# A two-layer encoder kernel: layer 1's side work spread differently over engines, queues and buffers

## The chip, the cores and the metric

The kernel runs on one core of a Trainium2 chip. The metric is the device time of one execution in microseconds (us); lower is better. Engines are named as in the profile: PE is TensorE's matmuls, PEld its weight loads, DVE is VectorE, ACT ScalarE, POOL GpSimd, and SP is SyncE, which here only issues DMAs; a "q" behind a name (SPq, ACTq) is the engine's own queue of such issues.

## The reference

The program is a trunk of two layers on x of shape 1 x 2048 x 1024. Layer 0 mixes two attentions (dilated and differential); the change does not touch it. Layer 1 is, cut to what matters:

```python
h = rms_norm(x, norm_g) * (1 + scale) + shift
q, k, v, g = split(h @ w_in, [1024, 1280, 1536])       # w_in: 1024 x 2560
y = banded_attention(q, k, v)                          # 16 heads, 4 key heads, |i-j| <= 128, sink logit, ALiBi
x = x + gate * ((y * silu(g)) @ w_out)
out = rms_norm(x, final_g)
```

Everything is float32. Each product of two float32 operands is made of three matmuls in a reduced format: an operand is split into a high part and a low part (the rest), and high x high, high x low and low x high are summed.

## The kernel before, in words

**Stages of layer 1.** The 2048 tokens are four blocks (b = 0 to 3) of 512, or 16 tiles (t) of 128. For a block, `layer1_norm` loads x, normalises it, `layer1_h` transposes it in eight chunks of 128 features (k = 0 to 7; L1083) and `modulate` (L267) makes the high and low halves of h: ACT evicts the transposed chunk from PSUM with scale and shift (hr, L271), POOL writes the high part (L272), DVE the low part (L273). `layer1_qkv` (L1096) then projects in 11 pieces: two of k, one of v, eight of q; `layer1_gate` (L1109) has eight pieces of the gate. `proj_pieces` (L331) is a Python generator that gives control back after every step; for a k, q or gate piece a step is one chunk k, that is the three matmuls of `three` (L292) over 512 columns.

**Weights.** Each piece loads its 128 columns of w_in (`wr`, two buffers), ACT writes the high part (L342) and DVE, or POOL for odd pieces, the low part (L343). The v piece has 256 columns in two halves, both with the low part on POOL (L352). One piece is prepared ahead.

**Sinks.** A finished k or q piece goes through `split` (ACT high, DVE low) into tiles of the tag `ev` (four buffers) and is stored to HBM by two DMAs on SP (L397); v through L434 to L436, also into `ev`; the gate through a tanh on ACT and a DVE multiply, stored to `G1[b]` (L426).

**Attention** is done by tile t: `load_attend` brings K, V and Q back from HBM on SP (L1145 to L1159). A tile has four groups of four heads: scores (L603, L604), row maximum on DVE (L1184) and its product with the slope (nm, L1188), exp on ACT (L1191); then, one group later, transposes (L1199), the split of the transposed weights into hC and lC (for the middle key tile on POOL, L1206 and L1207, else ACT and DVE) and the products with V (L1219). At a tile's end y is scaled: a row of factors goes through HBM (L1249, L1252), POOL multiplies all of y in one instruction (L1254), and SP stores it to `yC[t]` (L1255).

**Order on TensorE.** Within this stage TensorE's order is written out by hand (`tc.manual_schedule`); the other engines' orders come from the framework's planner, which works from the order of the program and a simulated time. Each third of a head group is followed by some steps of a generator `filling`, at a rate that spreads n steps over the tiles (`parts_of`, L1326). While tiles of block b are attended, the filling is the gate of block b, then h and qkv of block b+1. `next_block` (L1310) orders the latter:

```python
next(norm)
for _ in norm:
    yield
    next(qkv)
    yield
```

so each transposed chunk is followed by the first qkv piece's matmuls on it. For block 3 the filling is its gate, then the gate of block 0, whose h is reloaded from HBM (16 loads, L1115); 76 steps of these 128 are spread over the attention, the rest comes behind it. PSUM has two buffers for transposes and projections together (`psj`, tag `mm`). h tiles have 20 buffers of the tag `hk`, where a block needs 16.

**Output.** `layer1_out` (L1057) goes through t = 0 to 15: y and G1 are loaded (L1004, L1006), multiplied on POOL (L1007), split, and multiplied with w_out, whose high and low halves stay in SBUF. w_out is loaded in 256 KB pieces (`load_wout`, L972): two chunks during the last attention tile, the other six (`wor1b`, `wor1c`) when the first output tile asks for them, on SP. The first two tiles take their terms in three parts, for the weights come in that order. Then the residual, the last norm and the store.

Of the kernel before, what the change touches and what calls it, by code (L numbers as in the profile page):

```python
# [21 lines left out]
P = 128  # L22
# [12 lines left out]
def f32(ap):  # L35
    return ap.bitcast(F32)
# [45 lines left out]
def tile_encoder(ctx: ExitStack, tc: tile.TileContext, x, c, ada_w, ada_b, norm_g, ab_w_in, ab_w_out,  # L82
# [248 lines left out]
    def proj_pieces(pool, ps, w, h, b, pieces, name, ahead=0):  # L331
# [4 lines left out]
        def weights(n):  # L336
            c0, sink_T, _ = pieces[n]
            if sink_T is not None:
                wr = pool.tile([P, KC, P], F32, name=f"wr_{name}_{b}_{n}", tag="wraw", bufs=2)
                nc.sync.dma_start(wr, w[:, c0:c0 + P].rearrange("(k p) f -> p k f", p=P))  # L340
                wt = pool.tile([P, 2, KC, P], FR, name=f"wt_{name}_{b}_{n}", tag="wt", bufs=2)
                nc.scalar.activation(wt[:, 0], wr, AF.Copy)  # L342
                (nc.gpsimd if n % 2 else nc.vector).tensor_tensor(wt[:, 1], wr, f32(wt[:, 0]), op=OP.subtract)  # L343
                return wt
            hi = pool.tile([P, KC, CH], FR, name=f"wh_{name}_{b}_{n}", tag="wt", bufs=2)
            lo = pool.tile([P, KC, CH], FR, name=f"wl_{name}_{b}_{n}", tag="wt", bufs=2)
            for i in range(2):
# [4 lines left out]
                nc.gpsimd.tensor_tensor(lo[:, ks], wr, f32(hi[:, ks]), op=OP.subtract)  # L352
# [40 lines left out]
    def sink_heads(pool, dst, scale, name, classes=None):  # L393
# [663 lines left out]
    def layer1_out(pool, ps, w, parts):  # L1057
        fg = row_bcast(pool, final_g.rearrange("(a d) -> a d", a=1), "fg")

        def finish(t, xt):  # L1060
# [6 lines left out]
                 by_k(lambda t: G1[t // 4][:, t % 4 * P:(t % 4 + 1) * P]), x1d, finish)  # L1067
# [15 lines left out]
    def layer1_h(pool, ps, b, xs, h, keep):  # L1083

        for k in range(KC):
            for part in h:
                part.append(pool.tile([P, 512], FR, name=f"h1T{b}_{len(part)}_{part is h[1]}", tag="hk", bufs=20))
# [8 lines left out]
    def layer1_qkv(pool, ps, h, b, qs):  # L1096
# [7 lines left out]
        pieces = [(D + f * P, sink_heads(pool, k_rows(f), 1.0, f"kc{f}"), None) for f in range(2)]  # L1104
        pieces.append((D + CH, None, sink_v(pool, lambda t: vC[b][t % 4 * P:(t % 4 + 1) * P], 64, "vc")))
        pieces += [(f * P, sink_heads(pool, q_rows(f), qs[:, f:f + 1], f"qc{f}"), None) for f in range(8)]
        return proj_pieces(pool, ps, c_w_in, h, b, pieces, "l1", 1)

    def layer1_gate(pool, ps, h, b):  # L1109
        if h is None:  # L1110
            h = [[pool.tile([P, 512], FR, name=f"h1G{b}_{i}_{k}", tag="hk", bufs=20) for k in range(KC)]
                 for i in range(2)]
            for k in range(KC):
                for i in range(2):
                    nc.sync.dma_start(f32(h[i][k]), hD1[i, :, k])  # L1115
# [47 lines left out]
    def attend(pool, ps, t, V, consts, loaded):  # L1163
# [73 lines left out]
        def end():  # L1237
# [16 lines left out]
            nc.gpsimd.tensor_tensor(y, y, F, op=OP.mult)  # L1254
            nc.sync.dma_start(yC[t], y)  # L1255
# [15 lines left out]
    with sbuf("pO") as pool_:  # L1271
# [8 lines left out]
        with sbuf("pO2") as pool2, psum("psO") as ps_:  # L1280
# [4 lines left out]
            pj = Bufs(right.enter_context(sbuf("pJ", side="right")), ev=4, wraw=2)  # L1285
# [14 lines left out]
    with sbuf("pC") as pool, psum("psC") as ps_:  # L1300
# [3 lines left out]
        with tc.manual_schedule(engines={nc.tensor.engine}):  # L1304
# [5 lines left out]
            def next_block(b):  # L1310

                h, xs = [[], []], layer1_norm(pj, b)
                norm, qkv = layer1_h(pj, psj, b, xs, h, False), layer1_qkv(pj, psj, h, b, qs)

                def go():
                    next(norm)
                    for _ in norm:
# [24 lines left out]
            for b in range(TB):  # L1342
                ts = range(max(4 * b - 1, 0), 4 * b + 3 if b < TB - 1 else NT)
                fills, n = [], 0
                if 0 < b < TB - 1:
                    fills, n = [layer1_gate(pj, psj, h1, b)], 64
                if b + 1 < TB:
                    h2, go = next_block(b + 1)
                    fills.append(go)
                    n += 8 + 96  # L1350
# [3 lines left out]
                filling, at = chain(*fills), [0, 0]  # L1354
# [23 lines left out]
    with sbuf("pZ") as pool, psum("psZ") as ps_:  # L1378
# [36 lines left out]
```

## Time and profile before

| | us |
|---|---|
| median of three runs | 3093.2 |
| lowest and highest run | 3083.75, 3102.27 |
| the profiled execution's own time | 3081.09 |
| its span, first to last instruction | 3079.2 |
| busy in the span: PE, DVE, ACT, POOL | 2789.2, 1947.1, 1495.6, 1141.1 |
| mean granted TensorE clock, of full speed | 0.964 |

The profile is of one execution; its rows give times from the start of the span. "busy" is the time in which an engine worked on an instruction. A matmul counts as busy also when the clock is halved, so a stretch loses time in two ways: PE idle, and PE busy at a granted clock under 1.00 (full speed is 2.4 GHz, the other level 1.2 GHz).

### The profile page before, as it was taken

What the parts mean: (1) busy time and instruction counts of PE and PEld (TensorE: products, weight loads), DVE (VectorE), ACT (ScalarE), POOL (GpSimd) and SP (SyncE); (2) the same over time, 40 slices, a digit from 0 to 9 for tenths busy, and PEclk for the clock granted to TensorE, in tenths of its full rate; (3) what the DMA queues carried; (4) which work ended last, traced back from release to release, by engine and by line L of the source; (5) the groups of instructions that cost most, each with busy time, mean ns of one, the idle gap of its engine ahead of it and who ended that gap; (6) DMA issues with size and microseconds to landing.
All of it is one profiled execution on the core that took longest, in us unless ns stands there. A gap on an engine that the chain in (4) does not pass through costs nothing. (4 is left out here: it accounts for less than half of the span.)

```text
span 3079.2 us, 43802 instructions
## 1 busy us (share of the span) xinstructions
PE 2789.2 (91%) x15056; PEld 2349.6 (76%) x15056; DVE 1947.1 (63%) x4248; ACT 1495.6 (49%) x2841; POOL 1141.1 (37%) x755
## 2 busy tenths in 40 slices
PE   6999799999999998899898888998898998988898
PEld 6788788888888887677776666786786886876686
DVE  7425276777776688755556766534685674777476
ACT  5311255556555556455556762222565664666221
POOL 3200175654746544222424332322333333344221
PEclk9999999999999999999999898999999998999899
DMA  6687743654645550398777888787677675875554
GB/s 262 235 284 237 204 135 103 195 168 134 168 141 175 132 183 21 100 266 227 208 215 196 202 240 244 248 279 179 175 191 179 184 181 145 201 169 162 176 192 161
DMA packets 545624, 577.00 MB, mean 187 GB/s; under 512 B 31521, under 2 KB 420858, under 8 KB 539258
## 3 DMA queue, kind: packets, MB, share of 16 engines
q1 hardware_dynamic: 533562, 557.43, 63.2%
q10 hardware_dynamic: 11840, 16.78, 1.6%
q8 instruction: 119, 1.95, 0.3%
q14 instruction: 103, 0.84, 0.1%
HBM read 405.98 MB, written 168.08 MB: 186 GB/s over the span
## 5 line engine op out<-in xcount | busy, mean ns | idle before, releaser
L654 ACT ACTIVATE s<-s,nm 128x2048 f32<-128x2048 f32 x128 | 256.7, 2006 | 141.4 <-DVE nm L653 141.3
L660 POOL TENSOR_SCALAR s<-s,rr 128x1536 f32<-128x1536 f32 x64 | 122.4, 1913 | 342.8 <-DVE rr L658 237.3
L603 PE MATMUL pq<-kB,q 128*128 128x512 f32 x512 | 217.0, 424 | 31.4 <-DVE mx L648 17.9
L675 ACT ACTIVATE th<-pt 128x512 fp32r<-128x512 f32 x256 | 146.9, 594 | 176.6 <-PE pt L671 137.4
L663 POOL TENSOR_TENSOR s<-s,s 128x1536 f32<-128x1536 f32 x64 | 230.2, 3596 | 4.9
L1184 DVE CUSTOM_DVE_ANT_0 sC<-pqC,tabC,isl 128x384 f32<-128x384 f32 (+1 forms) x256 | 148.9, 596 | 112.9 <-PE pqC L604 111.6
L604 PE MATMUL pq<-kB,q 128*128 128x512 f32 x512 | 206.1, 402 | 0.0
L676 DVE TENSOR_TENSOR tl<-pt,th 128x512 fp32r<-128x512 f32 x256 | 170.4, 683 | 53.2 <-ACT th L675 53.0
L648 DVE CUSTOM_DVE_ANT_0 s<-pq,ndist 128x1024 f32<-128x1024 f32 x128 | 156.0, 1219 | 75.5 <-PE pq L604 53.9
L1191 ACT ACTIVATE sC<-sC,nmC 128x384 f32<-128x384 f32 (+1 forms) x256 | 152.2, 596 | 90.7 <-DVE nmC L1188 90.2
L648 DVE CUSTOM_DVE_ANT_0 s<-pq,ndist,mx 128x1024 f32<-128x1024 f32 x128 | 163.5, 1277 | 28.0 <-PE pq L604 25.3
L297 PE MATMUL py<-tl,vB 128*128 128x256 f32 x512 | 151.8, 297 | 14.4 <-DVE tl L676 13.8
L671 PE MATMUL pt<-ident,s 128*128 128x128 f32 x1024 | 152.4, 276 | 2.7 <-DVE s L661 2.3
L294 PE MATMUL py<-th,vB 128*128 128x256 f32 x512 | 149.8, 292 | 2.1 <-ACT th L675 2.0
L343 POOL TENSOR_TENSOR wt_g<-wr_g,wt_g 128x1024 fp32r<-128x1024 f32 x32 | 77.4, 2418 | 199.0 <-ACT wt_g L342 194.4
L294 PE MATMUL pp_l<-h1T_False,wt_l 128*128 128x512 f32 x320 | 135.2, 423 | 17.2 <-POOL h1T_False L272 13.1
L603 PEld LDWEIGHTS pq<-kB,q 128*128 128x128 f32 x512 | 98.7, 193 | 63.7 <-DVE mx L648 28.8
L298 PE MATMUL py<-th,vB 128*128 128x256 f32 x512 | 146.2, 285 | 0.0
L1007 POOL TENSOR_TENSOR yr<-yr,gr 128x512 f32<-128x512 f32 (+1 forms) x46 | 61.3, 1335 | 206.1 <-issue 49.3
L1199 PE MATMUL ptC<-ident,sC 128*128 128x128 f32 x736 | 115.4, 277 | 19.5 <-ACT sC L1191 19.1
L298 PE MATMUL pp_l<-h1T_False,wt_l 128*128 128x512 f32 x320 | 127.6, 399 | 5.1 <-POOL wt_l L343 5.1
L297 PE MATMUL pp_l<-h1T_True,wt_l 128*128 128x512 f32 x320 | 128.3, 401 | 4.2 <-DVE h1T_True L273 4.1
(417 smaller groups left out, 9128.6 us busy)
## 6 DMA issues: line engine op xcount, KB each, us to landing
wr_a<-in_ab_w_in_dram SPq DMA_DIRECT2D x48, 512.0 KB
wr_l<-in_c_w_in_dram SPq DMA_DIRECT2D x48, 512.0 KB
hD<-h0T SPq DMA_DIRECT2D x8, 2048.0 KB
aw_ss<-in_ada_w_dram SPq DMA_DIRECT2D x32, 512.0 KB
hs_a<-hD SPq DMA_DIRECT2D x16, 1024.0 KB
q<-qB SPq DMA_DIRECT2D x128, 128.0 KB
wr_g<-in_ab_w_in_dram SPq DMA_DIRECT2D x32, 512.0 KB
hs_g<-hD SPq DMA_DIRECT2D x16, 1024.0 KB
```

Source lines behind the costliest of these rows:

```text
L294: first = nc.tensor.matmul(pt, l[0], r[0], start=(k == 0), stop=False)
L297: nc.tensor.matmul(pt, l[0], r[1], start=False, stop=False)
L298: nc.tensor.matmul(pt, l[1], r[0], start=False, stop=(k == nk - 1))
L603: first = nc.tensor.matmul(ps_, q0, k0, start=True, stop=False)
L604: nc.tensor.matmul(ps_, q1, k1, start=False, stop=True)
L648: nc.vector.tensor_tensor_reduce(out=s_[:, half * 1024:(half + 1) * 1024], in0=pq, in1=ndist[:, o:o + 1024], scale=1.0, scalar=LOW if half ...
L654: nc.scalar.activation(s_, s_, AF.Exp, bias=nm, scale=slope_B(h), accum_out=lsum[:, a, t:t + 1])
L663: nc.gpsimd.tensor_tensor(Pm[0][:, W:], Pm[0][:, W:], Pm[1][:, W:], op=OP.add)
L671: nc.tensor.transpose(pt[:, kk, j], A[j][:, kb * P:(kb + 1) * P], ident)
L676: nc.vector.tensor_tensor(lo, src, f32(hi), op=OP.subtract)
L1184: nc.vector.tensor_tensor_reduce(out=Sx[r][:, :n], in0=pq[:, :n], in1=tab[:, o:o + n], scale=1.0, scalar=isl[:, h:h + 1], op0=OP.add, op1= ...
L1191: nc.scalar.activation(Sx[r][:, :n], Sx[r][:, :n], AF.Exp, bias=nm[:, h:h + 1], scale=slope_C(h), accum_out=ls[:, h:h + 1])
```

## The change

Layer 1 only. Low parts of weights go to DVE, but for the second half of v. The two stores of a k or q piece go to two queues (high on ACT, low on SP). The scaling of y is two POOL instructions, and its store goes to POOL's own queue. `ev` has six buffers for four, `wraw` three for two, `hk` 16 for 20. While a gate runs, its first seven pieces come first; then the chunks of the next block's transposes come in turns with the steps of the last gate piece, and the whole qkv behind them. In the last block 100 of the 128 gate steps are spread over the attention. The output goes through t = 4 to 15, then 0 to 3, and loads w_out's last six chunks on ACT's queue.

```diff
@@ proj_pieces
-                (nc.gpsimd if n % 2 else nc.vector).tensor_tensor(wt[:, 1], wr, f32(wt[:, 0]), op=OP.subtract)
+                (nc.gpsimd if n % 2 and not ahead else nc.vector).tensor_tensor(wt[:, 1], wr, f32(wt[:, 0]),
+                                                                                op=OP.subtract)
...
-                nc.gpsimd.tensor_tensor(lo[:, ks], wr, f32(hi[:, ks]), op=OP.subtract)
+                (nc.vector if ahead and not i else nc.gpsimd).tensor_tensor(lo[:, ks], wr, f32(hi[:, ks]),
+                                                                            op=OP.subtract)
@@ sink_heads (engs=(nc.scalar, nc.sync) for layer 1's k and q, (nc.sync, nc.sync) elsewhere)
-                nc.sync.dma_start(dst(i, b), f32(p))
+                engs[i].dma_start(dst(i, b), f32(p))
@@ layer1_out
-                 by_k(lambda t: G1[t // 4][:, t % 4 * P:(t % 4 + 1) * P]), x1d, finish)
+                 by_k(lambda t: G1[t // 4][:, t % 4 * P:(t % 4 + 1) * P]), x1d, finish,
+                 ts=chain(range(4, NT), range(4)))
@@ layer1_h, layer1_gate: tag="hk", bufs=20 -> 16; the reloaded h tiles are allocated in pairs, k by k
@@ attend, end()
-            nc.gpsimd.tensor_tensor(y, y, F, op=OP.mult)
-            nc.sync.dma_start(yC[t], y)
+            for ks in (slice(0, KC // 2), slice(KC // 2, KC)):
+                nc.gpsimd.tensor_tensor(y[:, ks], y[:, ks], F[:, ks], op=OP.mult)
+            nc.gpsimd.dma_start(yC[t], y)
@@ tile_encoder
-            pj = Bufs(right.enter_context(sbuf("pJ", side="right")), ev=4, wraw=2)
+            pj = Bufs(right.enter_context(sbuf("pJ", side="right")), ev=6, wraw=3)
...
+                    for n, _ in enumerate(gate or ()):
                         yield
-                        next(qkv)
-                        yield
+                        if n >= 56:
+                            next(norm)
+                            yield
+                    if not gate:
+                        next(norm)
+                        for _ in norm:
+                            yield
+                            next(qkv)
+                            yield
                     yield
                     yield from qkv
...
-                    fills, n = [layer1_gate(pj, psj, h1, b), layer1_gate(pj, psj, None, 0)], 64 + 12
+                    filling, n = chain(layer1_gate(pj, psj, h1, b), layer1_gate(pj, psj, None, 0)), 64 + 36
...
-        w = Rows((mid, lambda: wy), (last2, lambda: load_wout(pool, c_w_out, last2, raw, "1b")),
-                 (lower, lambda: load_wout(pool, c_w_out, lower, raw, "1c")))
-        layer1_out(pool, ps, w, lambda t: [mid, last2, lower] if t < 2 else [upper, lower])
+        w = Rows((mid, lambda: wy), (last2, lambda: load_wout(pool, c_w_out, last2, raw, "1b", 512, nc.scalar)),
+                 (lower, lambda: load_wout(pool, c_w_out, lower, raw, "1c", 512, nc.scalar)))
+        layer1_out(pool, ps, w, lambda t: [mid, last2, lower] if 4 <= t < 6 else [upper, lower])
```

For block 0 there is no gate, and the order of transposes and qkv stays as it was.

## Rows read from the trace of the kernel before

**Rows 1.** Windows of layer 1: stretch, length, busy (count) by engine, PEclk, DMA share, GB/s.

```profile
2131.20:2190.00 58.80, 38.81 (x226) 34.05 (x226) 22.38 (x63) 21.34 (x53) 15.14 (x10) 0.85 0.74 180
2332.00:2400.00 68.00, 51.67 (x295) 43.21 (x294) 34.04 (x80) 32.31 (x70) 26.65 (x22) 0.92 0.60 161
2400.00:2462.00 62.00, 62.00 (x316) 52.20 (x315) 42.82 (x96) 39.16 (x85) 21.32 (x16) 1.00 0.67 190
2534.00:2612.00 78.00, 61.14 (x329) 51.03 (x328) 36.34 (x90) 36.28 (x79) 28.52 (x24) 0.89 0.54 142
2680.00:2832.60 152.60, 133.72 (x708) 109.54 (x708) 118.28 (x321) 105.44 (x259) 60.76 (x50) 0.99 0.70 166
2832.60:2904.00 71.40, 58.20 (x209) 43.95 (x208) 25.50 (x32) 21.80 (x35) 14.57 (x9) 0.82 0.59 184
2904.00:3067.60 163.60, 163.52 (x722) 135.08 (x720) 117.83 (x285) 35.16 (x59) 38.05 (x29) 1.00 0.53 179
```

**Rows 2.** PE's waits, 2332 to 2400 us: us in total, times, longest.

```profile
PE pp_l L294 <- POOL h1T_False L272: 5.7, 2, 4.4
PE pn_l L297 <- POOL wl_l L352: 2.4, 1, 2.4
PE pt_h L265 <- ACT hr L271: 2.4, 3, 1.1
PE pt_h L265 <- DVE gg_g L425: 2.0, 1, 2.0
```

**Rows 3.** Timeline of POOL from 2334 us: start, us, instruction.

```profile
2334.42 2.34 POOL L1254 TENSOR_TENSOR yC<-yC,fC 128x1024 f32<-128x1024 f32 x1 [7.20 <-DMA fC<-fC]
2336.72 2.33 POOL L343 TENSOR_TENSOR wt_l<-wr_l,wt_l 128x1024 fp32r<-128x1024 f32 x1
2339.03 1.20 POOL L272 TENSOR_SCALAR h1T_False<-hr 128x512 fp32r<-128x512 f32 x2
```

**Rows 4.** Timeline of POOL and DVE, 2818 to 2823 us.

```profile
2818.41 2.37 POOL L1254 TENSOR_TENSOR yC<-yC,fC 128x1024 f32<-128x1024 f32 x1 [1.87 <-PE ptC L1199]
2818.82 1.97 DVE L1188 TENSOR_TENSOR nmC<-mxC,nsl 128x2 f32<-128x2 f32 x1
...
2820.74 2.31 POOL L1207 TENSOR_TENSOR lC<-rC,hC 128x512 fp32r<-128x512 f32 x1
```

**Rows 5.** Line L343 in layer 1: duration min/median/max in ns, first and last start.

```profile
L343 DVE TENSOR_TENSOR wt_g<-wr_g,wt_g x16: 1160/1218/1227, 2256.0 to 2859.5; 128x1024 fp32r<-128x1024 f32 x16
L343 POOL TENSOR_TENSOR wt_g<-wr_g,wt_g x16: 2385/2398/2797, 2263.6 to 2865.0; 128x1024 fp32r<-128x1024 f32 x16
```

**Rows 6.** ACT's waits in layer 1.

```profile
ACT vc L434 <- DMA kC<-hi_kc: 14.6, 1, 14.6
```

**Rows 7.** Timeline, 2131 to 2147 us: block 1's first k piece.

```profile
2131.68 0.60 ACT L386 ACTIVATE hi_kc<-pp_l 128x512 fp32r<-128x512 f32 x1 [2.25 <-PE pp_l L298]
...
2146.34 0.37 SPq L397 DMA_DIRECT2D kC<-hi_kc  x1
```

**Rows 8.** Windows: the same stretch's DMA engines (share 1.12).

```profile
2140.00:2160.00 20.00, 7.28 (x53) 6.84 (x53) 2.69 (x12) 3.36 (x13) 2.41 (x2) 0.73 1.12 279
```

**Rows 9.** PE's waits, 2680 to 2832.6 us.

```profile
PE pyC L1219 <- POOL lC L1207: 6.0, 4, 3.4
PE pyC L1219 <- POOL hC L1206: 5.5, 4, 2.1
```

**Rows 10.** PE's waits, 2832.6 to 2904 us.

```profile
PE po L294 <- ACT woh1b L981: 8.0, 1, 8.0
PE po L294 <- ACT woh1c L981: 2.4, 3, 1.1
```

**Rows 11.** Timeline of SP's queue at the start of the output.

```profile
2877.63 3.37 SPq L1006 DMA_DIRECT2D gr<-G  x3
2881.05 1.41 SPq L980 DMA_DIRECT2D wor1b<-in_c_w_out_dram  x3
```

**Rows 12.** Line L397 in layer 1: what one store's issue takes on SP, ns min/median/max.

```profile
L397 SPq DMA_DIRECT2D qC<-hi_qc x32: 319/329/2572, 2047.5 to 2673.2; - x32
```

More of the change, by code (lines that the diff above doesn't have):

```diff
@@ L391, in split, with sink_heads @@
         return hi, lo
[L393 removed]
+    def sink_heads(pool, dst, scale, name, classes=None, engs=(nc.sync, nc.sync)):
         def go(pt, b):
             for i, p in enumerate(split(pool, pt, f"{name}_{b}", scale)):
[L397 removed]
+                engs[i].dma_start(dst(i, b), f32(p))
                 if classes is not None:
@@ L1086, in layer1_h @@
             for part in h:
-                part.append(pool.tile([P, 512], FR, name=f"h1T{b}_{len(part)}_{part is h[1]}", tag="hk", bufs=20))
+                part.append(pool.tile([P, 512], FR, name=f"h1T{b}_{len(part)}_{part is h[1]}", tag="hk", bufs=16))
             pt = ps.tile([P, 512], F32, name=f"pt_h1_{b}_{k}", tag="t")
@@ L1102, in k_rows @@
             return lambda i, b: kC[b][i, 2 * f:2 * f + 2].rearrange("h f s -> (h f) s")
-        pieces = [(D + f * P, sink_heads(pool, k_rows(f), 1.0, f"kc{f}"), None) for f in range(2)]
+        pieces = [(D + f * P, sink_heads(pool, k_rows(f), 1.0, f"kc{f}", engs=(nc.scalar, nc.sync)), None) for f in range(2)]
         pieces.append((D + CH, None, sink_v(pool, lambda t: vC[b][t % 4 * P:(t % 4 + 1) * P], 64, "vc")))
-        pieces += [(f * P, sink_heads(pool, q_rows(f), qs[:, f:f + 1], f"qc{f}"), None) for f in range(8)]
+        pieces += [(f * P, sink_heads(pool, q_rows(f), qs[:, f:f + 1], f"qc{f}", engs=(nc.scalar, nc.sync)), None) for f in range(8)]
         return proj_pieces(pool, ps, c_w_in, h, b, pieces, "l1", 1)
@@ L1110, in layer1_gate @@
         if h is None:
-            h = [[pool.tile([P, 512], FR, name=f"h1G{b}_{i}_{k}", tag="hk", bufs=20) for k in range(KC)]
-                 for i in range(2)]
+            h = [[], []]
             for k in range(KC):
                 for i in range(2):
+                    h[i].append(pool.tile([P, 512], FR, name=f"h1G{b}_{i}_{k}", tag="hk", bufs=16))
                     nc.sync.dma_start(f32(h[i][k]), hD1[i, :, k])
@@ L1308, in tile_encoder, with projections @@
             before, pend = [], []
-            def next_block(b):
-                h, xs = [[], []], layer1_norm(pj, b)
-                norm, qkv = layer1_h(pj, psj, b, xs, h, False), layer1_qkv(pj, psj, h, b, qs)
+            def projections(b, gate):
+                h, xs = [[], []], layer1_norm(pj, b + 1)
+                norm, qkv = layer1_h(pj, psj, b + 1, xs, h, False), layer1_qkv(pj, psj, h, b + 1, qs)
                 def go():
-                    next(norm)
-                    for _ in norm:
+                    for n, _ in enumerate(gate or ()):
                         yield
-                        next(qkv)
-                        yield
+                        if n >= 56:
[7 more added lines that the diff above has]
+                            yield
                     yield
@@ L1343, in tile_encoder @@
                 ts = range(max(4 * b - 1, 0), 4 * b + 3 if b < TB - 1 else NT)
[L1344 to L1346 removed]
                 if b + 1 < TB:
[L1348 to L1354 removed]
+                    h2, filling = projections(b, layer1_gate(pj, psj, h1, b) if b else None)
+                    n = 104 + 64 * (b > 0)
+                else:
+                    filling, n = chain(layer1_gate(pj, psj, h1, b), layer1_gate(pj, psj, None, 0)), 64 + 36
+                at = [0, 0]
                 if b == 0:
```

## The prediction, made before the changed kernel was run

> **What bounds the kernel now.** I read the windows first. In a good stretch of layer 1 TensorE is the bound: from 2400 to 2462 us PE is busy in 62.00 of 62.00 us at clock 1.00 with attention and projection mixed, and in the output 722 matmuls take 163.60 us, 0.2266 us each [rows 1]. So time is to be had only where PE idles or runs at the half clock (1.2 of 2.4 GHz). I put a stretch's loss at its length less PE busy, plus its length times (1 - PEclk). That gives 20.0 + 8.8 = 28.8 us for stretch A (from 2131.2), 16.3 + 5.4 = 21.8 for B (2332), 16.9 + 8.6 = 25.4 for C (2534), 18.9 + 1.5 = 20.4 for D (2680) and 13.2 + 12.9 = 26.1 for E (2832.6) [rows 1]: 122.5 us in all. B and C are where a gate ends and the next block's h is made; A is the same for block 1, with the start of the attention; D is block 3's attention; E is the last gate steps and the start of the output. Then I asked the waits what ends the idle time in each, and the timeline why.
>
> **B and C: transposes in turns with the last gate piece.** In B, PE waits 5.7 us for the high part of h on POOL, 2.4 us for the eviction hr, 2.0 us for a PSUM buffer that the gate's sink still reads, and 2.4 us for the low part of v's weights [rows 2]; C's list is the same to within 0.6 us. POOL is late because two long instructions stand ahead of L272: the scaling of y (2.34 us) and a weight's low part (2.33 us) [rows 3]. In the new order POOL has the time of the last gate piece for the eight chunks, and only scaling halves of about 1.2 us can stand ahead: the 5.7 us goes. DVE makes a low part in 1.218 us where POOL takes 2.398 [rows 5], so of v's 2.4 us half goes, 1.2 us. The two halves of v's low part may also exclude one another (see D), and then it is longer: between 1.2 gained and 1.2 lost; I take the gain, as DVE's half comes first in the program. What stays: a gate piece holds one of the two PSUM buffers, so each transposed chunk still waits for the hr of the one before (2.4 us), and the first still for the gate's sink (2.0). What is new: the first qkv piece starts right behind the last gate piece and must wait for that one's sink too; nearest row 2.0 us [rows 2]. Net 5.7 + 1.2 - 2.0 = 4.9 us, and half of the 3.8 us of small waits outside the list, 1.9. The half clock follows the idle time; I let half of it go, 2.7 and 4.3 us. B gives 9.5, C 11.1: **21 us**. Bounds: 0, if the single PSUM buffer takes POOL's place; 38, if nothing stays of the 47.2 us but hr and the first sink.
>
> **A: two more `ev` buffers, high parts stored by ACT.** ACT waits 14.6 us before evicting block 1's first v tile, for the store of hi_kc [rows 6]: all four `ev` buffers hold k. The high part was begun at 2131.68, its store issued at 2146.34 [rows 7], as SP was issuing attention loads in between. With six buffers two v tiles go at once, and ACT issues the store when its own instruction is done. Late next: the piece behind v needs its weights, whose loads queue behind those same loads on SP. Nothing shows how far the stores then land sooner: the DMA engines are full there (share 1.12, [rows 8]). Bounds: 4 us (two v tiles early, then the same wait) and 23 (the 14.6 us and all of the 8.8 us at half clock). I take **12 us**, near the middle, as both rows have weight. SP is also rid of 16 y stores, 12 w_out loads and 40 of the 80 stores of k and q.
>
> **D: POOL rid of weights, y scaled in halves, more gate steps.** PE waits 6.0 + 5.5 us for lC and hC on POOL [rows 9]. While POOL scales y, DVE's tiny nm takes 1.97 us and ends with POOL's instruction; right after, lC takes 2.31 us on POOL (while DVE makes a low part): the two engines exclude each other [rows 4]. The longest instruction ahead of hC halves, from 2.4 to 1.2 us, so I take half of 11.5: **6 us**. DVE gets eight more low parts, 8 x 1.218 = 9.7 us, and with 24 more gate steps the stretch grows by 24 x 3 x 0.2266 = 16.3 us of matmuls; DVE's 118.28 of 152.60 us [rows 1] becomes (118.28 + 9.7) / 168.9 = 0.76 of the longer stretch, room enough. If all 9.7 us lay on the path, D would lose that; at best it gains its 20.4.
>
> The y store on POOL's queue has no row. Between SP's 0.33 us for an issue [rows 12] and 2.4 us, the longest POOL instruction [rows 5], the 16 cost 5 to 38 us of an engine that is busy 60.76 of 152.60 us; I take the small end and charge nothing, its cover being POOL's idle time. If it were the long end, it would stand ahead of hC as L343 did, and D's 6 us would be gone. The Trainium skill speaks against this edit (SBUF — State Buffer, SBUF: two separate sides): descriptors of a POOL-issued DMA are written by GpSimd, which some DVE instructions lock out. No run here shows it; by it the long end would hold.
>
> **E: output from t = 4, w_out on ACT's queue.** PE waits 8.0 and 2.4 us for the last six chunks of w_out [rows 10]. Their loads leave at 2881.05 behind loads of G1, which for t = 0 wait on the last gate's stores [rows 11]. Block 1's G1 has long been in HBM, and ACT's queue is not behind SP's, so the loads can start while the gate still runs. But 24 steps of cover, 16.3 us, have moved into D, and the loads share four `yh` buffers with the first tiles. Of the 10.4 us I keep 4, of 12.9 us at half clock 7, and take off 2 for the shorter cover: **10 us**. Bounds 0 and 20.
>
> **Costs beside the path.** ACT issues 40 stores and 12 loads, 52 x 0.329 = 17 us [rows 12], covered by its idle third (39.16 of 62.00 us busy, [rows 1]). With 16 `hk` buffers no h chunk of the last gate is loaded early; each has eight steps, 5.4 us of matmuls and the attention between, to come back. I charge nothing; if that cover fails, PE waits for h1G.
>
> **The sum:** 21 + 12 + 6 + 10 = 49 us. The profiled execution took 3081.1 us and would take 3032; it lies 12.1 us under the median of the runs, 3093.2, from which I forecast **3044 us**.
>
> **Rivals.**
> *The DMA engines, not the queues, are the limit.* For: share 1.12 while the k store waits [rows 8]. Against: 0.59 in E [rows 1]. Then A gives 4 and E 4: gain 35, 3058 us. The Trainium skill states it as a rule (DMA: Bandwidth & Descriptors, Issuing engines are not separate DMA queues): whoever issues, the same 16 engines carry it, and several issuers save only issue time. The share of 1.12 agrees.
> *One PSUM buffer.* In B and C the chunks wait for hr and sinks as long as they did for POOL. For: hr already costs 2.4 us [rows 2]. Against: the 5.7 us are POOL's. B and C give 5: gain 33, 3060 us.
> *Not what it says.* The planner orders DVE, ACT and the queues anew, and stalls of like size come up elsewhere: gain 10, 3083 us, no change.
> *Slower: ACT held by its DMA issues.* An issue has taken up to 2.57 us on SP where the rings were full [rows 12]; on ACT that holds the exps behind it, which TensorE's transposes wait for. At 2.24 us over the usual for each of 40 stores, all on the path, 90 us: 3134 us. It decides from (49 + 15.5) / 52 = 1.24 us per issue. Against: the median is 0.329.
>
> **How the numbers follow.** Chances: forecast 0.62, full DMA engines 0.13, PSUM 0.11, not what it says 0.08, ACT held 0.06. The measurement tells about 0.5%, 15.5 us. Under 3077.7 us lie the forecast and the first two rivals, less a little for their upper bounds: faster 0.84, same 0.10, slower 0.06. The range: 3014 is a gain of 79, some two thirds of the way from 49 to the sum of the upper bounds (38 + 23 + 20 + 20 = 101); 3080 takes in the first two rivals with their own low ends. Outside are the last two and the extremes.
>
> **What would show it.** B and C: no wait for h on POOL above 1 us, PE idle about 10 us each. A: ACT's 14.6 us wait gone, PE's loss under 18. D: waits for hC and lC halved. E: wor1b issued on ACT before the last gate piece ends, PE's wait under 4 us. Wrong would be: pt_h waiting for hr over 8 us a block, DVE busy over 0.9 of D, ACT's DMA issues over 1 us, or a wait for h1G.

## The result and the profile after

The changed kernel takes 3053.39 us in the median of four runs (3050.76 to 3054.89), the kernel before 3092.51 in the runs beside it (3083.75 to 3102.27). The ratio is 0.9872, with an interval of 0.9841 to 0.9903: faster by 1.3 %. The forecast was 3044 with a range of 3014 to 3080; the measured time lies 9.4 us above the forecast and 4.6 and 6.6 us under the two rivals at 3058 and 3060.

| profiled execution | before | after |
|---|---|---|
| own time, us | 3081.09 | 3051.91 |
| span, us | 3079.2 | 3050.1 |
| busy: PE, DVE, ACT, POOL | 2789.2, 1947.1, 1495.6, 1141.1 | 2787.7, 1945.4, 1495.9, 1064.8 |
| mean granted clock | 0.964 | 0.965 |

To see where 29.1 us of span went, both traces are cut at equal work, not at equal times. **A** runs from the first transposes of block 1 to the first gate matmul of block 1, **B** and **C** from there to the first gate matmul of blocks 2 and 3, **D** from there to the last gate matmul, **out** from there to the last matmul of the output; the rest is the end. First the windows of the kernel before, with the columns of [rows 1], then the same five after:

```profile
2115.30:2262.60 147.30, 121.62 (x645) 100.25 (x644) 86.46 (x245) 76.70 (x175) 46.43 (x39) 0.94 0.80 191
2262.60:2466.40 203.80, 187.47 (x984) 157.55 (x982) 132.84 (x316) 119.94 (x259) 75.36 (x57) 0.97 0.70 182
2466.40:2673.70 207.30, 190.44 (x984) 159.82 (x981) 130.23 (x313) 119.43 (x259) 76.14 (x57) 0.96 0.68 173
2673.70:2873.30 199.60, 178.33 (x900) 146.03 (x898) 137.01 (x348) 121.78 (x287) 75.32 (x57) 0.97 0.70 174
2873.30:3067.10 193.80, 182.99 (x771) 147.80 (x771) 129.29 (x301) 44.92 (x76) 41.95 (x33) 0.95 0.53 177
```

```profile
2115.00:2258.20 143.20, 125.74 (x646) 103.63 (x644) 84.65 (x253) 77.22 (x175) 38.03 (x38) 0.94 0.80 197
2258.20:2450.30 192.10, 184.56 (x984) 156.12 (x982) 133.87 (x323) 119.28 (x259) 58.23 (x55) 0.99 0.74 193
2450.30:2642.30 192.00, 185.21 (x982) 157.20 (x981) 132.28 (x323) 119.36 (x259) 57.20 (x55) 0.98 0.71 181
2642.30:2844.60 202.30, 183.03 (x901) 149.16 (x900) 132.37 (x357) 122.33 (x288) 61.07 (x62) 0.94 0.68 167
2844.60:3033.10 188.50, 181.76 (x771) 146.76 (x770) 124.61 (x288) 43.63 (x73) 42.33 (x32) 0.96 0.55 188
```

The matmul counts show that the work is equal in these two (a few records are missing). A gained 4.1 us, B 11.7, C 15.3, out 5.3; D lost 2.7 and the end 4.9 (12.1 before, 17.0 after). The gain is in B and C; D has a lower clock than before, 0.94 against 0.97, and its 2.7 us lie within the scatter of D, which the next section gives.

**B.** The waits of PE in B after the change, which answer to [rows 2]:

```profile
PE pt_h L265 <- ACT hr L271: 4.7, 3, 3.3
PE pn_l L297 <- DVE wl_l L353: 1.2, 1, 1.2
PE pp_l L298 <- DVE wt_l L343: 0.7, 1, 0.7
PE pp_l L294 <- ACT hr L271: 0.6, 1, 0.6
```

The 5.7 us on POOL and the 2.0 us for the gate's sink are gone; v's low part costs 1.2 us where it cost 2.4; the wait for hr has grown, from 2.4 to 4.7 us.

**A.** The timeline of ACT (ACTq: its DMA issues), which answers to [rows 7], and then SP's queue in the same microseconds:

```profile
2131.28 0.60 ACT L388 ACTIVATE hi_kc<-pp_l 128x512 fp32r<-128x512 f32 x1 [2.25 <-PE pp_l L298]
...
2143.23 0.33 ACTq L399 DMA_DIRECT2D kC<-hi_kc  x1
2143.66 0.60 ACT L388 ACTIVATE hi_kc<-pp_l 128x512 fp32r<-128x512 f32 x1 [9.88 <-DMA klC<-kC]
2149.19 0.33 ACTq L399 DMA_DIRECT2D kC<-hi_kc  x1
2149.84 0.51 ACT L1194 ACTIVATE sC<-sC,nmC 128x256 f32<-128x256 f32 x1 [5.59 <-DMA qC<-qC]
```

```profile
2130.42 0.61 SPq L1158 DMA_DIRECT2D klC<-kC  x1
2131.08 5.17 SPq L1162 DMA_DIRECT2D qC<-qC  x2
```

The 14.6 us of [rows 6] are gone, but the store of hi_kc, ready at 2131.88, is issued at 2143.23, and what ends that wait is the landing of klC, an attention load that *SP* issued at 2130.42. In the trace the DMAs of SP and ACT take turns on eight completion semaphores (each counts one DMA's landing), in planned order; the store and that load have the same one, and the issue waits until the load that last had it has landed. So ACT stands still 9.88 and 5.59 us at its own stores.

**D.** PE's waits in D, which answer to [rows 9], then POOL's timeline at one tile's end:

```profile
PE pyC L1222 <- POOL hC L1209: 11.2, 6, 5.0
PE pyC L1222 <- POOL lC L1210: 7.0, 6, 1.5
```

```profile
2780.64 2.84 POOL L1258 TENSOR_TENSOR yC<-yC,fC 128x512 f32<-128x512 f32 x2 [13.04 <-DMA fC<-fC]
2783.77 0.60 POOL L1259 DMA_DIRECT2D yC<-yC  x1 [0.30 <-POOL yC L1258]
2784.41 0.63 POOL L1209 TENSOR_SCALAR hC<-rC 128x512 fp32r<-128x512 f32 x1
2785.12 1.26 POOL L1210 TENSOR_TENSOR lC<-rC,hC 128x512 fp32r<-128x512 f32 x1
```

The number in brackets is the one to read: before the 2.84 us of work POOL idles 13.04 us for the row of factors that comes back by way of HBM, and hC of the next tile stands behind it in POOL's order, though its input has long been there: ACT wrote that rC before 2775.3, 9 us earlier.

```profile
2774.64 0.58 ACT L1208 ACTIVATE rC<-ptC 128x512 f32<-128x512 f32 x1
```

**Out.** The first w_out loads on ACT's queue with the instruction of ACT's ahead of them, and the window of the first 27 us of the output:

```profile
2843.94 0.42 ACT L1012 ACTIVATE yh<-yr 128x256 fp32r<-128x256 f32 x1 [2.87 <-POOL yr L1009]
2843.95 0.97 ACTq L982 DMA_DIRECT2D wor1b<-in_c_w_out_dram  x2
2850.36 0.63 ACT L983 ACTIVATE woh1b<-wor1b 128x512 fp32r<-128x512 f32 x1 [4.30 <-DMA gr<-G]
```

```profile
2844.60:2872.00 27.40, 20.66 (x61) 13.28 (x60) 11.96 (x19) 9.40 (x16) 3.31 (x4) 0.75 0.74 245
```

The loads leave 0.65 us before the last gate matmul, where [rows 11] had them after the loads of G1. In ACT's order they stand behind the split of the first output tile (yh), which waits for POOL's product, and that for rows that SP loads once the attention is over. Still PE idles 6.7 of these 27.4 us, the granted clock is 0.75 in the mean, and PE's waits, which answer to [rows 10], are these:

```profile
PE po L294 <- ACT woh1b L983: 4.3, 3, 2.9
PE po L294 <- ACT woh1c L983: 2.2, 4, 0.9
```

### The profile page after: what moved, and what is told of

Same layout as the page of the kernel before. It is cut to its first block, busy times and chain, and to the rows that moved or that the text cites. A ratio compares the mean times of both kernels' runs of the same rounds, so it can differ in the third digit from the quotient of the medians.

```text
span 3050.1 us, 43740 instructions
## 1 busy us (share of the span) xinstructions
PE 2787.7 (91%) x15056; PEld 2348.1 (77%) x15056; DVE 1945.4 (64%) x4288; ACT 1495.9 (49%) x2841; POOL 1064.8 (35%) x747
## 5 line engine op out<-in xcount | busy, mean ns | idle before, releaser
L1187 DVE CUSTOM_DVE_ANT_0 sC<-pqC,tabC,isl 128x384 f32<-128x384 f32 (+1 forms) x256 | 148.5, 596 | 138.5 <-PE pqC L606 137.8
L677 ACT ACTIVATE th<-pt 128x512 fp32r<-128x512 f32 x256 | 146.8, 593 | 174.9 <-PE pt L673 135.1
L297 PE MATMUL py<-tl,vB 128*128 128x256 f32 x512 | 152.2, 297 | 14.1 <-DVE tl L678 13.4
L1209 POOL TENSOR_SCALAR hC<-rC 128x512 fp32r<-128x512 f32 x64 | 42.8, 668 | 324.0 <-ACT rC L1208 298.4
L673 PEld LDWEIGHTS pt<-ident,s 128*128 128x128 f32 x1024 | 120.7, 142 | 8.7 <-DVE s L663 2.7
```

The source lines that it names most:

```text
L297: nc.tensor.matmul(pt, l[0], r[1], start=False, stop=False)
L673: nc.tensor.transpose(pt[:, kk, j], A[j][:, kb * P:(kb + 1) * P], ident)
L1187: nc.vector.tensor_tensor_reduce(out=Sx[r][:, :n], in0=pq[:, :n], in1=tab[:, o:o + n], scale=1.0, scalar=isl[:, h:h + 1], op0=OP.add, op1= ...
```

## The experiments

Each kernel was profiled once and cut in the same way; us. The kernel before, run beside each of them, has medians of 3092.5 to 3100.0, so the kernels compare best by their ratio to it:

| kernel | A | B | C | D | out | end | median of its runs | ratio |
|---|---|---|---|---|---|---|---|---|
| before | 147.3 | 203.8 | 207.3 | 199.6 | 193.8 | 12.1 | 3092.5 | 1 |
| changed | 143.2 | 192.1 | 192.1 | 202.3 | 188.5 | 17.0 | 3053.4 | 0.9872 |
| e1 old order of transposes | 141.8 | 202.0 | 202.1 | 204.0 | 190.6 | 12.9 | 3070.9 | 0.9927 |
| e2 low parts on GpSimd | 152.2 | 195.1 | 194.5 | 209.0 | 188.0 | 14.0 | 3069.6 | 0.9931 |
| e3 high stores on SP | 139.7 | 191.1 | 191.0 | 201.1 | 188.0 | 13.4 | 3052.8 | 0.9876 |
| e4 y scaled later | 134.7 | 190.4 | 191.8 | 179.8 | 188.9 | 13.5 | 3023.7 | 0.9784 |
| e5 output from t = 0 | 141.3 | 191.7 | 191.1 | 199.4 | 193.6 | 13.5 | 3060.2 | 0.9881 |
| e6 w_out on SP | 143.6 | 191.3 | 190.1 | 202.8 | 186.7 | 13.8 | 3049.3 | 0.9844 |
| e7 64 + 12 gate steps | 143.1 | 191.5 | 192.2 | 202.9 | 176.2 | 12.1 | 3045.8 | 0.9823 |
| e8 y scaled and stored as before | 137.3 | 190.4 | 191.2 | 198.5 | 190.9 | 14.2 | 3043.4 | 0.9829 |
| c1 e4, SP stores, 8 buffers | 129.4 | 191.9 | 191.6 | 184.1 | 189.4 | 13.8 | 3023.9 | 0.9760 |
| f1 e4 with 64 + 12 | 137.8 | 190.4 | 191.5 | 189.0 | 178.0 | 11.6 | 3021.9 | 0.9750 |
| f2 f1, SP stores, 8 buffers | 129.9 | 191.6 | 190.4 | 187.8 | 176.6 | 10.7 | 3016.6 | 0.9722 |
| f3 f1, GpSimd stores | 125.7 | 191.7 | 190.4 | 187.7 | 177.0 | 11.3 | 3011.9 | 0.9717 |

In five kernels the cuts do not bound equal work. In e2, twenty matmuls of layer 0's output fall behind block 1's first transposes and so into A; in e7, f1, f2 and f3, 14 or 15 matmuls of the output stand ahead of the last gate matmul and so in D, some 3.3 us at 0.2266 us each, and are missing from out. The windows of e2's A and e7's D, where the changed kernel has x646 and x901:

```profile
2113.80:2266.00 152.20, 131.65 (x665) 107.51 (x664) 87.76 (x250) 77.18 (x175) 47.58 (x43) 0.93 0.76 187
2651.80:2854.70 202.90, 183.90 (x915) 150.53 (x914) 141.61 (x363) 126.07 (x294) 63.35 (x64) 0.96 0.72 187
```

How far single executions scatter: A in the changed kernel, e1, e5, e6 and e7, where nothing of A differs, lies between 141.3 and 143.6, but e4 and f1, which have the same A too, differ by 3.1; B in all of the five but e1 lies between 191.3 and 192.1, D in the changed kernel, e1, e5 and e6 between 199.4 and 204.0, and out, with the code of the changed kernel (e1 to e4, c1, e8), between 188.0 and 190.9. The first transposes of block 1, which stand for the end of layer 0, the same everywhere, start between 2115.0 and 2128.4 (e2 aside), and that goes into every median.

**e1: the order alone undone.**

```diff
-                    for n, _ in enumerate(gate or ()):
-                        yield
-                        if n >= 56:
-                            next(norm)
-                            yield
-                    if not gate:
-                        ...
+                    yield from gate or ()
+                    next(norm)
+                    for _ in norm:
+                        yield
+                        next(qkv)
+                        yield
```

> The changed kernel, but with the transposes of a block back behind the whole gate and in turns with the first piece of its projections, as the kernel before had them; all else as changed. Stretches are measured between equal work: A from the first transposes of block 1 to the first gate piece of block 1, B and C from gate piece to gate piece (blocks 1, 2, 3), D from the first gate piece of block 3 to the last gate step, out from there to the last product of the output. In the changed kernel they take 143.2, 192.1, 192.0, 202.3 and 188.5 us; B and C took 203.8 and 207.3 before, so 27.0 us of gain lie there. Theory (the order made most of that gain): B and C together 15 to 27 us longer than in the changed kernel, A, D and out within 2 us, the time 0.5 to 0.9 % above the changed kernel's. Rival (it was GpSimd's relief from the weights' low parts): B and C together lose less than 8 us.

B and C lose 20.0 us together (9.9 and 10.0), A, D and out change by 2.1 us at most; ratio to before 0.9927 (0.9900 to 0.9955). The theory holds. PE's waits in B:

```profile
PE pp_l L294 <- POOL h1T_False L272: 5.4, 2, 4.4
PE pt_h L265 <- DVE gg_g L427: 1.9, 1, 1.9
```

These are the waits of [rows 2], back to 0.3 us, although POOL makes no low parts of weights here but half of v's. So the order removed them, not POOL's relief. Whether the old order would still cost as much with e4's later scaling of y, no run shows.

**e2: the low parts alone undone.**

```diff
-                (nc.gpsimd if n % 2 and not ahead else nc.vector).tensor_tensor(wt[:, 1], wr, f32(wt[:, 0]),
+                (nc.gpsimd if n % 2 else nc.vector).tensor_tensor(wt[:, 1], wr, f32(wt[:, 0]),
-                (nc.vector if ahead and not i else nc.gpsimd).tensor_tensor(lo[:, ks], wr, f32(hi[:, ks]),
+                nc.gpsimd.tensor_tensor(lo[:, ks], wr, f32(hi[:, ks]),
```

> The changed kernel, but with the low parts of the weights back on GpSimd where the kernel before had them (odd pieces and both halves of the v piece); all else as changed. The other half of the same question. Theory (the order made most of the gain of B and C): B and C together lose 2 to 10 us, as the transposes no longer stand in the pieces' way, but the 2.4 us operations still delay hC and lC now and then. Rival (GpSimd's relief): B and C together lose 15 to 27 us. If both parts together are needed, this run and the one with the old order each lose most of the 27 us.

B and C lose 5.4 us, as the theory had it; but A and D lose too, which neither had. D loses 6.7. Of A's 9.0 us the twenty matmuls of layer 0 take more than 4; at equal work A loses 4 to 6 (147.0 for 143.1 us from the last matmul of layer 0, 146.8 for 141.1 from the first projection of block 1). So the low parts on DVE are worth some 16 to 18 us in all, as the medians have it (16.2), and most of it lies outside B and C. PE's waits in D:

```profile
PE pyC L1222 <- POOL hC L1209: 13.1, 6, 5.0
PE pyC L1222 <- POOL lC L1210: 8.8, 6, 3.6
```

**e3: the high parts' stores back on SP.**

```diff
-        pieces = [(D + f * P, sink_heads(pool, k_rows(f), 1.0, f"kc{f}", engs=(nc.scalar, nc.sync)), None) for f in range(2)]
+        pieces = [(D + f * P, sink_heads(pool, k_rows(f), 1.0, f"kc{f}"), None) for f in range(2)]
```

(and the same for q.)

> The changed kernel, but with the stores of the high parts of q and k back on SyncE's queue; six buffers and all else as changed. Theory (in A, ScalarE is held by the store that it issues, as that store waits for a load that SyncE issued earlier): the ScalarE waits of 9.88 and 5.59 us at 2143 and 2149 are gone, and with them some 6 us of TensorE's waits; A is 4 to 8 us shorter than 143.2, the other stretches within 3 us each. Rival (the wait moves with the store to SyncE, behind which the next loads then stand): A within 2 us of 143.2 or longer, and B and C together 0 to 10 us longer.

A is 3.5 us shorter, between the two, and little more than the 3.1 by which e4 and f1 differ; the median does not move. ACT's waits at its own stores are gone, and a wait for a buffer is back, 8.2 us where [rows 6] had 14.6:

```profile
ACT vc L436 <- DMA kC<-hi_kc: 8.2, 1, 8.2
```

With six buffers that wait is shorter; it does not end, as SP issues hi_kc late.

**e4: y scaled later.** POOL's order within the attention stage is written out by hand, and a tile's scaling and store stand behind the third group of the next tile. In A and D nothing else of POOL's order differs from the changed kernel; in B and C one pair of hC and lC and v's low part also stand elsewhere.

```diff
+            def scale():
+                for ks in (slice(0, KC // 2), slice(KC // 2, KC)):
+                    nc.gpsimd.tensor_tensor(y[:, ks], y[:, ks], F[:, ks], op=OP.mult)
+                nc.gpsimd.dma_start(yC[t], y)
+
+            late.append(scale)
...
                     nc.gpsimd.tensor_tensor(lo, raw, f32(hi), op=OP.subtract)
+                    if kv == 2 and late:
+                        late.pop()()
...
-        with tc.manual_schedule(engines={nc.tensor.engine}):
+        with tc.manual_schedule(engines={nc.tensor.engine, nc.gpsimd.engine}):
```

> The changed kernel, but with GpSimd's scaling of a tile's y and its store put behind the third group of the next tile (GpSimd's order written out by hand, as TensorE's is); the work is the same. Theory (in D, hC and lC are late because GpSimd waits in order for the factors that come back by way of DRAM, 8.7 to 13 us at each tile, and not because its operations are long): GpSimd's waits for fC go from 50.5 us to under 10, TensorE's waits for hC and lC in D from 18.2 us to under 6, D from 202.3 to 187 to 193 us, and B and C are together 0 to 6 us shorter; the time 0.3 to 0.6 % under the changed kernel's. Rival (TensorE's waits in D are of the clock and of the thinner work, and another wait takes their place): D within 3 us of 202.3.

D is 22.5 us shorter, more than expected, and A 8.5; B and C change by 2.0. The median is 3023.7, the ratio to before 0.9784 (0.9759 to 0.9809). PE's waits for POOL in D, then D's window:

```profile
PE pyC L1226 <- POOL lC L1212: 0.6, 1, 0.6
```

```profile
2639.00:2818.80 179.80, 174.65 (x900) 144.07 (x899) 138.63 (x357) 122.17 (x288) 62.73 (x62) 0.98 0.76 190
```

18.2 us of waits became 0.6. PE idles 5.2 us where it idled 19.3, which is 14.1 of the 22.5; the other 8.4 are PE's busy time, 183.03 to 174.65 for the same matmuls, as the clock went from 0.94 to 0.98. Each microsecond of waiting had cost some 0.6 more in clock; by c1 below it is 0.9, as there 9.7 us of idle time and 8.5 of busy time are gone from D.

**e5 to e7: the output.** Three parts undone one by one.

```diff
@@ e5
-                 by_k(lambda t: G1[t // 4][:, t % 4 * P:(t % 4 + 1) * P]), x1d, finish,
-                 ts=chain(range(4, NT), range(4)))
+                 by_k(lambda t: G1[t // 4][:, t % 4 * P:(t % 4 + 1) * P]), x1d, finish)
-        layer1_out(pool, ps, w, lambda t: [mid, last2, lower] if 4 <= t < 6 else [upper, lower])
+        layer1_out(pool, ps, w, lambda t: [mid, last2, lower] if t < 2 else [upper, lower])
@@ e6
-        w = Rows((mid, lambda: wy), (last2, lambda: load_wout(pool, c_w_out, last2, raw, "1b", 512, nc.scalar)),
+        w = Rows((mid, lambda: wy), (last2, lambda: load_wout(pool, c_w_out, last2, raw, "1b")),
...
@@ e7
-                    filling, n = chain(layer1_gate(pj, psj, h1, b), layer1_gate(pj, psj, None, 0)), 64 + 36
+                    filling, n = chain(layer1_gate(pj, psj, h1, b), layer1_gate(pj, psj, None, 0)), 64 + 12
```

> The changed kernel, but with the output in the old order of token blocks (from block 0 on, whose gate is the last one computed); all else as changed, w_out still loaded on ScalarE's queue. In the changed kernel the output takes 188.5 us from the last gate step to its last product, and 17.0 us from there to the end. Theory (the new order spares the wait for the last gate's way through DRAM at the start, and gives part of it back at the end, where VectorE lags): the output 3 to 6 us longer, the end after the last product 12 to 14 us, the time 0 to 3 us above the changed kernel's. Rival (the order is what brought the 5.3 us of the output, and the lag at the end has another cause): the output 3 to 6 us longer, the end still 16 to 18 us, the time 3 to 6 us above. Second rival (the loads of w_out are late anyway and hide the gate's way): the output within 1.5 us.

> The changed kernel, but with the loads of w_out for the output back on SyncE's queue; the order of token blocks and all else as changed. Theory (ScalarE's queue issues them when the gate ends, where SyncE's queue stands at loads that wait for the gate): the output 3 to 8 us longer than 188.5, with TensorE's waits for woh1b and woh1c near the 10.4 us of before against 6.5 us. Rival (from block 4 on nothing on SyncE's queue waits for the gate any more, so the queue does not matter): the output within 1.5 us of 188.5, and the two parts of the change would then have bought the same few us twice.

> The changed kernel, but with 64 + 12 instead of 64 + 36 gate steps spread over the attention of the last block, so that 24 steps (16 us of TensorE) go back behind it; all else as changed. D took 202.3 us, 182.2 of them to the last sum transpose and 20.1 behind it. Theory (in D GpSimd's wait for the factors sets the pace at each tile, and the extra steps only filled TensorE while it lasted): to the last sum transpose 168 to 176 us, behind it 40 us, D in all 4 to 12 us longer than 202.3, as the steps now leave the waits bare. Rival (the extra steps did nothing for D): D within 3 us of 202.3.

In e5 the output takes 5.1 us longer, with one wait of 9.1 for woh1b. ACT's queue does not spare it: the loads stand behind ACT's split of the first tile, which here needs the last gate:

```profile
2856.57 0.42 ACT L1012 ACTIVATE yh<-yr 128x256 fp32r<-128x256 f32 x1 [7.30 <-POOL yr L1009]
2856.58 1.37 ACTq L982 DMA_DIRECT2D wor1b<-in_c_w_out_dram  x3
```

Its end is 13.5 us, as the theory said, but so it is, between 10.7 and 14.2, in every other kernel here, e1 to e3 with the same output code among them: the changed kernel's 17.0 belongs to that one execution, and nothing shows that the change caused it. In e6 the output is 1.8 us *shorter* (the rival had at most 1.5 either way): ACT's queue bought nothing. e7 shows the cost. Its theory missed: D is no longer without the 24 steps (202.9 for 202.3, and 15 matmuls of the output are in it), as the rival said; but what neither had, the output is 12.3 us shorter, and D and the output together 11.7. The first 27 us behind the gate, and the first loads, which leave 18 us before the gate's end at 2854.8:

```profile
2854.70:2882.00 27.30, 24.18 (x100) 18.11 (x99) 16.54 (x31) 9.21 (x16) 5.87 (x5) 1.00 0.54 170
```

```profile
2836.72 0.91 ACTq L982 DMA_DIRECT2D wor1b<-in_c_w_out_dram  x2
```

100 matmuls fit where 61 did, at full clock. In the changed kernel, e5 and e7 alike the first loads leave within 0.01 us of the second yh, whose rows SP loads behind the attention; so the gate steps behind the attention are what hides them, and the change took 24 of them away.

**e8: the scaling and store of y undone.**

```diff
-            for ks in (slice(0, KC // 2), slice(KC // 2, KC)):
-                nc.gpsimd.tensor_tensor(y[:, ks], y[:, ks], F[:, ks], op=OP.mult)
-            nc.gpsimd.dma_start(yC[t], y)
+            nc.gpsimd.tensor_tensor(y, y, F, op=OP.mult)
+            nc.sync.dma_start(yC[t], y)
```

> The changed kernel, but with y scaled in one GpSimd instruction and stored on SyncE's queue, as before; all else as changed. D took 202.3 us in the changed kernel, 199.6 before; the low parts alone were worth 6.7 us there (with them back on GpSimd D took 209.0), the spread of the gate steps 0.6. Theory (the store on GpSimd's queue, 0.60 us between hC and lC, is what cost D about 9 us): D 193 to 197 us, TensorE's waits for hC and lC from 18.2 to under 12 us. Rival (the wait for the factors is what counts, it is as long as before, and halves or store change it little): D within 3 us of 202.3, the waits for hC and lC 15 to 21 us; what D lost then is the other attention work that no longer fits beside the wait.

D is 3.8 us shorter, between the theory and the rival and 0.9 outside the scatter; A is 5.9 shorter, 4.0 outside it. POOL's order differs in nothing but the scaling and the store. The waits in D:

```profile
PE pyC L1222 <- POOL hC L1209: 10.5, 6, 3.9
...
PE pyC L1222 <- POOL lC L1210: 3.8, 4, 1.5
```

PE waits for hC as before, for lC 3.2 us less: in the changed kernel a store of 0.60 us stands ahead of lC at five tiles of D. The edit of y cost a little; it gained nothing. Halves and store were undone together, so their parts are not told apart.

**The version that beats both.** All four have e4's later scaling, and f1, f2 and f3 also e7's 64 + 12 steps. c1 and f2 take the high parts' stores to SP with eight `ev` buffers and two `wraw`; f3 issues them from POOL.

```diff
@@ c1, f2: stores on SP as in e3, and
-            pj = Bufs(right.enter_context(sbuf("pJ", side="right")), ev=6, wraw=3)
+            pj = Bufs(right.enter_context(sbuf("pJ", side="right")), ev=8, wraw=2)
@@ f3
-engs=(nc.scalar, nc.sync)
+engs=(nc.gpsimd, nc.sync)
```

> The kernel with GpSimd's scaling put later (which took 3023.7 us), and in addition the high parts' stores on SyncE's queue with eight store buffers instead of six, the third weight buffer given up for them (the same SBUF). Theory (in A the change traded a wait for a buffer against a wait of ScalarE at its own store; with the store off ScalarE and two more buffers both are gone): ScalarE has no wait over 4 us between the first transposes of block 1 and the first gate piece but the one for the first transpose, A goes from 134.7 to 128 to 131 us, the other stretches within 2 us. Rival (the data is late, not the engine: K and V of the next tiles must land anyway, and TensorE's first steps in A stay bound by that): A within 2 us of 134.7. Second rival (the third weight buffer was needed): B and C together 3 to 10 us longer than 382.2.

> The kernel with GpSimd's scaling put later (3023.7 us) and the 24 gate steps back behind the attention (64 + 12). Theory (the 24 steps spread over the attention buy nothing there and uncover the loads of w_out, for which the steps behind the attention are the cover; this adds to the later scaling): the output 175 to 178 us instead of 188.9, D 178 to 182 us instead of 179.8, the time 3009 to 3014 us, 0.3 to 0.5 % under the later scaling alone. Rival (with GpSimd's wait gone, the thinner attention of the last block becomes bound by the chain from scores to products): D 4 to 10 us longer, the time 3015 to 3021 us.

> The same, and the high parts' stores on SyncE's queue with eight store buffers and two weight buffers. A took 129.4 us so against 134.7, and D 184.1 against 179.8. Theory (both differences belong to the stores): A 128 to 131 us, D 3 to 5 us longer than with the stores on ScalarE, the time within 3 us of that of the kernel with 64 + 12 and the later scaling alone. Rival (the 4 us of D were one late load in one execution): 4 to 6 us less than that kernel.

> The same as the kernel with 64 + 12 and the later scaling, with the high parts' stores issued by GpSimd instead of ScalarE, six store buffers and three weight buffers as in the changed kernel. Theory (the store holds ScalarE because its issue waits in ScalarE's order, and costs nothing where nobody's next work stands behind it): ScalarE's waits of 9.6 and 5.7 us near the start of A are gone, A is 4 to 6 us shorter than 134.7, B, C and D within 2 us. Rival (GpSimd is held instead, some 10 us at a time, and hC and lC come late): TensorE's waits for hC and lC come back, A, B, C and D together 5 to 20 us longer.

c1: A falls to 129.4 as expected, D rises by 4.3, where one wait for an exp takes 3.6 us, and the median does not move. f1: the rival holds. Of the 10.9 us that the output gains D gives 9.2 back. The 14 matmuls of the output that moved into D are some 3.2 of these; the rest is what the 24 steps, gone from D, had filled: PE idles 9.0 us there for 5.2 in e4, and its waits for an exp are 7.5 us for 2.6. f2: A 129.9, and D is not longer than in f1, so c1's 4.3 us look like that execution's; 3016.6 against 3021.9 for f1. f3: A is 125.7, 9.0 under e4 and 12.1 under f1; ACT's two waits at its stores are gone, and the stores that POOL issues count on eight semaphores of POOL's own. B, C and D stay within 1.3 us of f1. Its window of A, and the 20 us that lie where [rows 8] lie, counted from A's start:

```profile
2124.10:2249.80 125.70, 118.52 (x645) 98.27 (x643) 86.19 (x250) 77.36 (x175) 43.19 (x47) 0.99 0.88 221
2148.80:2168.80 20.00, 17.28 (x130) 15.95 (x129) 11.84 (x36) 12.17 (x33) 4.97 (x6) 0.97 1.12 313
```

Against A of the changed kernel the same loads and stores go through the same DMA engines at a higher share, 0.88 for 0.80, and PE idles 7.2 us for 17.5. In the 20 us the share is the 1.12 of [rows 8] again, but PE is busy 17.28 us for 7.28 before: what was waited for, and where, held A back, and not the engines. f3 takes 3011.9 us (3006.0 to 3015.5), ratio to before 0.9717 (0.9691 to 0.9744); f2 and f3 cannot be told apart by their times.

## Why the prediction came out right, and which steps did not

**The time came out within the range though three terms of four were off.** By stretches the sum was 21 + 12 + 6 + 10 = 49; measured, 27.0 for B and C, 4.1 for A, -2.7 for D and 5.3 - 4.9 for out and end, and 0.3 before A: 29.1. The medians differ by 39.1, for the profiled execution of before lay 11.4 us under its median and that of after 1.5. So the two medians flatter the sum by some 10 us of scatter, and B and C made good 6 of the 26 us that the other three terms fell short: that the time lies near the forecast is in part luck. (E's terms, 4 + 7 - 2, make 9 and not the 10 of the sum.) Of the prediction's own signs two failed: PE's waits for hC and lC rose from 11.5 to 18.2 us instead of halving, and its wait for w_out is 6.5 us and not under 4.

**B and C: right, mis-sized.** The waits for h on POOL are gone, v's low part went from 2.4 to 1.2, and hr is still waited for, all as forecast. PE idles 7.5 and 6.8 us there, where some 10 were forecast. The 2.0 us charged for a wait of the first qkv piece for the gate's sink did not come, and the old one, which was to stay, went too, while the wait for hr grew by 2.3 in B; and in C the granted clock rose from 0.96 to 0.98, in B from 0.97 to 0.99. e1 puts 20.0 of it down to the order, e2 5.4 to the low parts; together 25.4 of 27.0.

**A: the step "ACT issues the store when its own instruction is done" failed.** It issues it 11.4 us later, when a load of SP's has landed. The rival in which ACT is held by its issues named the right place and the wrong price. It put the 2.57 us of its longest issue down to full rings; the DMA share is 1.15 there (2190 to 2200 us), but no row shows a ring's fill. What holds ACT is the wait ahead of the issue, not the issue, which answers to [rows 12] with

```profile
L399 ACTq DMA_DIRECT2D qC<-hi_qc x24: 326/326/343, 2179.8 to 2641.7; - x24
```

By e3 that edit cost A some 3.5 us; by e8 the edit of y cost it 5.9; what gained was the low parts, 4 to 6, which the prediction had not counted in A at all, and, if the parts add up, the buffers, left with some 8, which no run undoes alone. The measure of loss was wrong as well. On the prediction's own stretch it falls from 28.8 to 16.7 us (58.80 - 49.12 idle, and 0.12 of 58.80 for the clock), as its sign asked:

```profile
2130.90:2189.70 58.80, 49.12 (x263) 42.72 (x262) 26.90 (x82) 26.49 (x65) 11.07 (x9) 0.88 0.81 201
```

But the stretch holds only 37 more matmuls, some 6 us at the pace of the rest of A before (419 in 72.6 us). A microsecond that is idle and at the half clock counts one and a half times in that measure, though a low clock costs nothing while PE idles. The rival of full DMA engines also said 4 us for A, and for a wrong reason: by f3 the same transfers allow 125.7. The Trainium skill's rule behind that rival (DMA: Bandwidth & Descriptors, Issuing engines are not separate DMA queues) says that whoever issues, the same engines carry it, and that a second issuer saves only the issue's time. No run speaks against the first half; on the second the trace disagrees: the issue is a third of a microsecond, and who issued decided what stood behind its wait, 9.0 us of A between e4 and f3, where f1's longer A makes it 12.1.

**D: the step "The longest instruction ahead of hC halves, from 2.4 to 1.2 us, so I take half of 11.5" failed.** The two halves run back to back in 2.5 to 3.0 us, and what stands ahead of hC is not the instruction but POOL's wait for its factors, 60.1 us in six waits, to be seen in [rows 3] already as the bracket of 7.20 us, which I read past. e4 moves that wait alone and gains 22.5. That the 9.7 us of low parts on DVE lie beside other work fits: DVE is busy 132.37 of 202.30 us, and in e2, without them, D is not shorter but 6.7 us longer. The y store on POOL, charged at nothing between 5 and 38, took 0.60 us each:

```profile
L1259 POOL DMA_DIRECT2D yC<-yC x16: 602/602/731, 2209.9 to 2837.0; - x16
```

16 x 0.602 = 9.6 us of POOL. So the Trainium skill's warning (SBUF — State Buffer, SBUF: two separate sides) did not show as a long issue here. But the store stands ahead of lC, and by e8 that and the halves cost D up to 3.8 us. Why D is 9.4 us longer in e2 than before is only in part told by that: the store on ACT (1.2), y (3.8) and the gate steps (2.8, with e7's 15 matmuls of the output taken out) leave some 2 us open, and each of the three lies within D's scatter or close to it.

**E: "take off 2 for the shorter cover" failed.** The cover cost 11.7 us in D and the output together (e7). So did "ACT's queue is not behind SP's, so the loads can start while the gate still runs": on ACT they stand behind a split that waits for loads of SP's, and left only 0.65 us ahead of the last gate matmul. The order from t = 4 was worth 5.1 (e5; 2.7 by the scatter of out at the least), the queue nothing (e6). The end's loss looks like scatter.

## What to carry to other kernels

Read the bracket before the instruction: where an in-order engine idles for a round trip through HBM, halving its work changes nothing, and moving the work behind what could already run was worth the wait and the clock lost with it (22.5 us of D). A store costs the engine that issues it what it waits for, not what the issue takes; look at who stands behind it. Before moving filler work into a busy stage, name what it hides where it is. And count a low clock only over the time in which TensorE works.

## What was not expected of the hardware

A wait cost more than its length: with 14.1 us of idle time gone in D, 8.4 us of busy time for the same matmuls went too, as the granted clock rose from 0.94 to 0.98 (e4). And a store that ACT issued waited 11.4 us for the landing of a load that SP had issued, through the turns that both take on one set of completion semaphores; stores on POOL's queue, at about 0.6 us each and on semaphores of their own, had no such wait in f3.
